# The head of a four-layer trunk: first transfers in small ordered pieces, squares later, constant products on TensorE first

## The chip, the cores and the metric

One Trainium2 chip, of which the kernel uses one core. The metric is the device time of one execution in microseconds (us), the median of several runs. TensorE multiplies matrices (its row is PE in the profile, and PEld for its loads of weights), VectorE (DVE) and ScalarE (ACT) do elementwise work, GpSimd (POOL) makes masks, SyncE (SP) issues most transfers.

## The reference

Two layers (`DEPTH = 2`) over 256 tokens of width 1024, all in float32. Each layer is a half-step SwiGLU, a mixer of three branches (sparse attention, pooling, state-space scan), a second half-step SwiGLU and an embedding gate. Only the start of the first half-step matters here:

```python
def rmsnorm(x, g):
    x32 = x.astype(jnp.float32)
    y = x32 * lax.rsqrt(jnp.mean(x32 * x32, axis=-1, keepdims=True) + EPS)
    return (y * g.astype(jnp.float32)).astype(x.dtype)

def swiglu(x, w_gate, w_up, w_down):
    return (jax.nn.silu(x @ w_gate) * (x @ w_up)) @ w_down

    h = x
    for i in range(DEPTH):
        h = h + 0.5 * swiglu(rmsnorm(h, ffn1_norm[i]), ffn1_w_gate[i], ffn1_w_up[i], ffn1_w_down[i])
        ...
    return rmsnorm(h, final_norm)
```

## The kernel before

The state `h` lies transposed, as 8 pieces of 128 channels x 256 tokens. A float32 product is made of three products of shortened numbers: every operand is split into a rounded part `hi` (ScalarE casts) and the rest `lo` (VectorE subtracts), and `mm3` (L161) issues hi x hi, lo x hi, hi x lo. The split activations are `uh` and `ul` (L187, L188), the split weights `whi` and `wlo` (L140, L141).

Weights come in units of 128 x 1024 numbers (512 KB). A unit has three buffers: `raw` (4 in turn), where the transfer lands, and `whi`, `wlo` (5 in turn each). So the transfer of unit n waits until the split of unit n-4 has read its `raw`, and the cast of unit n waits until TensorE is done with unit n-5. I count units from 0. One unit is 8 steps of `mm3`, 24 matmuls of 256 columns; units 2f and 2f+1 (gate and up) fill the two halves of one PSUM bank of `mm`, and there are 4 such banks, so the first matmul of unit 8 waits until the bank of units 0 and 1 has been read: once by `t = mm * r` (L369) and once more, after ScalarE's tanh (L371), by `t = t * mm` (L373).

The factor `r` of the norm comes aside: the squares of `h` are summed into `acc` (L218, L221, L223), TensorE sums `acc` over the channels with a product with `ones` (into `aux`), VectorE takes the inverse root in a chain of small operations (L250, `rsqrt` at L190) and writes two scaled identities (L256, L257), TensorE spreads them with `onesr` into another `aux`, and ScalarE copies that to `rs_r` (L267). Only then can a bank of `mm` be read. In the first half-step, matmuls run ahead of `r`.

In `build` (L1081) the first transfers are issued from SP: `h` in parts of 2, 2 and 4 pieces, and the first unit in two halves between them (`first`, L145); the two tables of gains `cc` go out from ScalarE's queue in `constants`. The squares of the first norm are asked for in `ffn` by `rnorm(late=True)` (L226). Within an engine, instructions are executed in the order of its queue. That order is made when the program is built, by a scheduler with its own estimate of times; `keep_in_program_order` holds an instruction to the order of the code, `turn` and `high_priority` push others.

Of the kernel before, what the change touches and what calls it, by code (L numbers as in the profile page):

```python
# [9 lines left out]
F = mybir.dt.float32  # L10
FR = mybir.dt.float32r
I32 = mybir.dt.int32
AF = mybir.ActivationFunctionType
OP = mybir.AluOpType
AX = mybir.AxisListType

P = 128
D = 1024
S = 256
DEPTH = 2  # L20
KD = D // P
# [24 lines left out]
NCC = -(-_n // 32) * 32  # L46
# [18 lines left out]
class Builder:  # L65
# [76 lines left out]
                                          op=OP.subtract))  # L142
        return hi, lo

    def first(self, c):  # L145

        nc = self.nc
        if c == 4:
            self.made.append(self.load(*self.order[1]))
            return  # L150
        if c == 0:
            self.start = self.parts()
            self.made.append(self.start[1:])
        layer, u, n = self.order[0]
        s = slice(0, 512) if c == 0 else slice(512, n)
        raw, hi, lo = self.start
        nc.sync.dma_start(raw[:, s], self.ins["w"][layer, u, :, s])
        nc.scalar.copy(hi[:, s], raw[:, s])  # L158
        nc.vector.tensor_tensor(lo[:, s], raw[:, s], hi[:, s].bitcast(F), op=OP.subtract)

    def mm3(self, ps, a, b, start, stop, keep=False):  # L161

# [47 lines left out]
            self.turn(nc.vector.scalar_tensor_tensor(y[:, :n], t[:, :n], 1.5, y[:, :n],  # L210
                                                     op0=OP.add, op1=OP.mult))

    def square(self, c, src, add=True):

        nc = self.nc
        if c == 0:
            self.acc = self.t([P, S], tag="acc", bufs=2)
            nc.scalar.activation(self.acc, src, AF.Square)  # L218
            return
        sq = self.t([P, S], tag="t1")  # L220
        nc.scalar.activation(sq, src, AF.Square)  # L221
        if add:
            nc.vector.tensor_tensor(self.acc, self.acc, sq, op=OP.add)  # L223
        else:
            self.last_sq = sq

    def rnorm(self, late=False, gap=1):

        nc = self.nc
        r = self.t([P, S], tag="rs_r", bufs=2)
        v = self.t([P, 2], tag="rs_v", bufs=2)
        rc = self.t([P, 8], tag="rs_y", bufs=2)
        acc = None if late else self.acc

        def steps():
            nonlocal acc
            if late:
                for c in range(KD):  # L240
                    self.square(c, self.h[:, c])
                    if c % 4 == 3:
                        yield
                acc = self.acc
            with self.tc.high_priority(offset=160):
                ps = self.bank("aux")
                for h in range(2):
                    self.mm(ps[:, h:h + 1], acc[:, h * P:(h + 1) * P], self.ones[:, :1],
                                     start=True, stop=True)
                self.turn(nc.vector.tensor_scalar(v, ps[:, :2], 1.0 / D, EPS, op0=OP.mult,  # L250
                                                  op1=OP.add))
                self.rsqrt(rc, v, 2)
                dh, dl = (self.t([P, 2, P], FR, tag="t1") for _ in range(2))
                for h in range(2):
                    x = rc[:, h:h + 1]
                    self.turn(nc.vector.tensor_scalar(dh[:, h], self.ident, x, None, op0=OP.mult))  # L256
                    self.turn(nc.vector.scalar_tensor_tensor(dl[:, h], self.ident, x,  # L257
                                                             dh[:, h].bitcast(F), op0=OP.mult,
                                                             op1=OP.subtract))
            for _ in range(gap):  # L260
                yield
            pr = self.bank("aux")
            for i, d in enumerate((dh, dl)):
                self.mm(pr[:, :S], self.onesr, d.rearrange("p a b -> p (a b)"),
                                 start=(i == 0), stop=(i == 1))
            with self.tc.high_priority(offset=160):
                nc.scalar.copy(r, pr[:, :S])  # L267

        self.todo = steps()
        return rc, r  # L270

# [5 lines left out]
    def constants(self):  # L277
        nc = self.nc
        c = self.const
        self.ident = c.tile([P, P], F, name="ident")  # L280
        self.ones = c.tile([P, P], F, name="ones")
        self.tri = c.tile([P, P], F, name="tri")
        self.up = c.tile([P, P], F, name="up")

        self.after = c.tile([P, 4, P], mybir.dt.bfloat16, name="after")
        nc.gpsimd.memset(self.ones, 1.0)
        nc.gpsimd.affine_select(out=self.ident, in_=self.ones, pattern=[[-1, P]],
                                compare_op=OP.is_equal, fill=0.0, base=0, channel_multiplier=1)

        nc.gpsimd.affine_select(out=self.tri, in_=self.ones, pattern=[[1, P]],  # L290
                                compare_op=OP.is_ge, fill=0.0, base=0, channel_multiplier=-1)
        nc.gpsimd.affine_select(out=self.up, in_=self.ones, pattern=[[-1, P]],
                                compare_op=OP.is_gt, fill=0.0, base=0, channel_multiplier=1)
        for i in range(4):
            nc.gpsimd.affine_select(out=self.after[:, i], in_=self.ones, pattern=[[1, P]],
                                    compare_op=OP.is_gt, fill=0.0, base=0, channel_multiplier=-1)
        self.onesr = c.tile([P, P], FR, name="onesr")
        nc.vector.tensor_copy(self.onesr, self.ones)

        warm = self.t([P, 1], tag="warm", bufs=1)  # L300
        nc.gpsimd.memset(warm, 0.0)
        nc.scalar.activation(warm, warm, AF.Tanh)
        self.cc = []
        for i in range(DEPTH):
            cc = c.tile([P, NCC], F, name=f"cc{i}")
            nc.scalar.dma_start(cc, self.ins["cc"][i])
            self.cc.append(cc)

    def col(self, layer, name, i=0, n=1):
        k = CC[name] + i  # L310
# [29 lines left out]
    def ffn(self, layer, u0, nxt, aside=None):  # L340
        nc = self.nc
        first = layer == 0 and u0 == U_FFN1
        _, r = self.rnorm(late=first, gap=3 if first else 2)
        gh = self.a([P, KF, S], FR, "gh")
        gl = self.a([P, KF, S], FR, "gl")
# [735 lines left out]
    def build(self):  # L1081
        nc = self.nc
        self.constants()
        self.h = self.const.tile([P, KD, S], F, name="h")
        self.a([P, LINE // 8], F, "shift")
        self.new_u()
        for c in range(KD):
            if c in (0, 2, 4):
                n = (2, 0, 2, 0, 4)[c]
                nc.sync.dma_start(self.h[:, c:c + n], self.ins["x"][:, c:c + n])  # L1090
                if self.order:
                    self.first(c)
            self.prep(c, 0, "ffn1_norm", False)
        for i in range(DEPTH):
            self.ffn(i, U_FFN1, (i, "mix_norm"))
            self.mix(i, (i, "ffn2_norm"))
            self.ffn(i, U_FFN2, (i, "ple_norm"), self.per_layer(i))
            self.ple(i, (i + 1, "ffn1_norm") if i + 1 < DEPTH else None)
# [109 lines left out]
```

## Time and profile before

| | us |
|---|---|
| median of 3 runs (1331.26 to 1332.53) | 1332.47 |
| the profiled execution | 1331.12 |
| its span, first to last instruction | 1329.4 |
| TensorE busy | 1308.3 |
| start of the first matmul | 6.62 |

The profiled execution took 1.35 us less than the median and 1.7 us more than its span. TensorE is busy in 98% of the span, so what counts is where it starts, waits, or runs at a lower clock. Times in the rows are from the start of the span.

### The profile page before, as it was taken

How to read it: one execution, taken by the hardware profiler on the slowest of the kernel's cores; microseconds unless marked ns; L12 is line 12 of the kernel's file. 1: busy time of each engine (PE TensorE's matmuls, PEld its weight loads, DVE VectorE, ACT ScalarE, POOL GpSimd, SP SyncE). 2: the span in 40 equal slices, each digit the busy share in tenths (PEclk: the TensorE clock that was granted, in tenths of full speed). 3: DMA queues.
4: the chain of work that ended last, by engine and by line, in shares of the span. 5: the costliest groups of instructions: out<-in, count | busy, mean ns of one | idle time of the engine just before them, and what ended most of it. 6: DMA issues, size and time to landing. Idle time of an engine off the chain costs nothing.

```text
span 1329.4 us, 28282 instructions
## 1 busy us (share of the span) xinstructions
PE 1308.3 (98%) x11502; PEld 1297.2 (98%) x11502; DVE 1040.5 (78%) x1971; ACT 740.9 (56%) x1209; POOL 7.0 (1%) x17
## 2 busy tenths in 40 slices
PE   7999999999999999999999999999999999999997
PEld 7999999999999999999999999999999999999997
DVE  7877659987989777766887776699789888777666
ACT  6555446656764555544645554566577546554454
POOL 0000000000000000000000000000000000000000
PEclk9999999999999999999999999999999999999999
DMA  7666656566637566666556666456655466666661
GB/s 255 209 193 193 192 168 206 159 203 195 188 122 230 159 222 191 193 194 197 187 164 192 193 194 196 155 195 192 198 187 163 151 207 206 193 195 198 193 192 47
DMA packets 72385, 248.24 MB, mean 187 GB/s; under 512 B 7936, under 2 KB 10304, under 8 KB 72256
## 3 DMA queue, kind: packets, MB, share of 16 engines
q1 hardware_dynamic: 71392, 245.17, 60.1%
q8 instruction: 90, 1.47, 0.5%
q10 hardware_dynamic: 864, 1.28, 0.3%
q14 instruction: 39, 0.32, 0.1%
HBM read 245.33 MB, written 1.08 MB: 185 GB/s over the span
## 4 chain that ended last, share of the span: by engine, by line
PE 95%; DVE 2%; DMA 1%; ACT 1%; issue 0%; DVEq 0%; ACTq 0%
PE mm L164 30%; PE mm L166 29%; PE mm L165 29%; PE aux L106 3%; PE aux L165 1%; PE aux L166 1%; DMA t<-in_p_dram 1%; PE aux L164 1%; PE aux L109 1%; DVE wlo L141 0%; ACT whi L140 0%; DMA h<-in_x_dram 0%; DVE ul L188 0%; DVE acc L223 0%; ACT uh L187 0%
## 5 line engine op out<-in xcount | busy, mean ns | idle before, releaser
L140 ACT CAST whi<-raw 128x1024 fp32r<-128x1024 f32 (+1 forms) x457 | 476.2, 1045 | 487.5 <-issue 234.6
L164 PE MATMUL mm<-uh,whi 128*128 128x256 f32 x2550 | 707.1, 279 | 8.7 <-ACT whi L158 6.6
L166 PE MATMUL mm<-uh,wlo 128*128 128x256 f32 x2560 | 709.2, 278 | 1.5 <-DVE wlo L141 1.5
L165 PE MATMUL mm<-ul,whi 128*128 128x256 f32 x2560 | 708.4, 277 | 0.4 <-DVE ul L188 0.3
L141 DVE TENSOR_TENSOR wlo<-raw,whi 128x1024 fp32r<-128x1024 f32 (+1 forms) x457 | 551.9, 1213 | 195.8 <-ACT whi L140 192.6
L164 PEld LDWEIGHTS mm<-uh,whi 128*128 128x128 f32 x2550 | 479.1, 189 | 11.5 <-ACT whi L158 6.6
L166 PEld LDWEIGHTS mm<-uh,wlo 128*128 128x128 f32 x2560 | 482.1, 188 | 2.8 <-DVE wlo L141 2.2
L165 PEld LDWEIGHTS mm<-ul,whi 128*128 128x128 f32 x2560 | 482.5, 189 | 1.1 <-DVE ul L188 1.1
L166 PE MATMUL mm<-gh,wlo 128*128 128x256 f32 x704 | 194.1, 276 | 0.0
L165 PE MATMUL mm<-gl,whi 128*128 128x256 f32 x704 | 194.1, 276 | 0.0
L164 PE MATMUL mm<-gh,whi 128*128 128x256 f32 x704 | 193.7, 276 | 0.0
L166 PEld LDWEIGHTS mm<-gh,wlo 128*128 128x128 f32 x704 | 132.1, 188 | 0.0
L165 PEld LDWEIGHTS mm<-gl,whi 128*128 128x128 f32 x704 | 132.1, 188 | 0.0
L164 PEld LDWEIGHTS mm<-gh,whi 128*128 128x128 f32 x704 | 131.8, 188 | 0.0
L165 PE MATMUL mm<-a,whi 128*128 128x256 f32 x256 | 70.3, 276 | 0.0
L164 PE MATMUL mm<-a,whi 128*128 128x256 f32 x256 | 70.2, 276 | 0.0
L166 PE MATMUL mm<-a,wlo 128*128 128x256 f32 x256 | 69.9, 277 | 0.0
L164 PEld LDWEIGHTS mm<-a,whi 128*128 128x128 f32 x256 | 47.9, 188 | 0.0
L165 PEld LDWEIGHTS mm<-a,whi 128*128 128x128 f32 x256 | 47.9, 188 | 0.0
L166 PEld LDWEIGHTS mm<-a,wlo 128*128 128x128 f32 x256 | 47.6, 188 | 0.0
L369 DVE TENSOR_TENSOR t<-mm,rs_r 128x256 f32<-128x256 f32 x88 | 37.3, 423 | 10.5 <-PE mm L166 0.9
L374 DVE SCALAR_TENSOR_TENSOR t<-t,t 128x256 f32<-128x256 f32 x88 | 37.4, 425 | 3.0
(213 smaller groups left out, 1106.0 us busy)
## 6 DMA issues: line engine op xcount, KB each, us to landing
raw<-in_w_dram SPq DMA_DIRECT2D x447, 512.0 KB, 4.2
gh<-rates SPq DMA_DIRECT2D x16, 256.0 KB, 4.4
raw<-in_w_dram SPq DMA_DIRECT2D x8, 352.0 KB, 3.0
raw<-in_w_dram SPq DMA_DIRECT2D x4, 256.0 KB, 3.8
gh<-rates SPq DMA_DIRECT2D x8, 128.0 KB, 3.6
h<-in_x_dram SPq DMA_DIRECT2D x2, 256.0 KB, 4.1
h<-in_x_dram SPq DMA_DIRECT2D x1, 512.0 KB, 5.7
t<-in_p_dram ACTq DMA_DIRECT2D x2, 256.0 KB, 5.8
```

What stands on the lines that cost most here:

```text
L106: self.tc.keep_in_program_order(self.nc.tensor.matmul(*args, **kw))
L109: self.tc.keep_in_program_order(self.nc.tensor.transpose(*args))
L140: nc.scalar.copy(hi[:, :n], raw[:, :n])
L141: self.turn(nc.vector.tensor_tensor(lo[:, :n], raw[:, :n], hi[:, :n].bitcast(F), op=OP.subtract))
L164: (self.mm if keep else mm)(ps, a[0], b[0], start=start, stop=False)
L165: mm(ps, a[0], b[1], start=False, stop=False)
L166: mm(ps, a[1], b[0], start=False, stop=stop)
L369: nc.vector.tensor_tensor(t, p1[0], r, op=OP.mult)
L374: nc.vector.scalar_tensor_tensor(g, th, 1.0, t, op0=OP.add, op1=OP.mult)
```

## The change

The transfers of the first 4 us are cut into a list, `HEAD`, of ten pieces: single pieces of `h` (128 KB) and then pairs, and units 0 and 1 in parts of 256 and 512 columns. `head` issues them in that order, from SP except the first weights, which go out from ScalarE's queue beside 32 columns of `cc` (the gains of the first norm); the rest of `cc` follows after the ten. The casts and splits are held to the same order on ScalarE and VectorE. The squares are held to the code's order, which puts them behind these. 15 products of the constant `onesr` with itself stand first in TensorE's queue; nothing reads their result.

```diff
-    def first(self, c):
-        ...
+    HEAD = (("x", 0, 1), ("w", 0, 0, 256), ("x", 1, 1), ("w", 0, 256, 512), ("x", 2, 2),
+            ("w", 0, 512, 1024), ("x", 4, 2), ("x", 6, 2), ("w", 1, 0, 512), ("w", 1, 512, 1024))
+
+    def head(self, layer, gain):
+        nc = self.nc
+        keep = self.tc.keep_in_program_order
+        units = [self.parts() for _ in range(2)] if self.order else []
+        self.made = [u[1:] for u in units]
+        for k, (what, i, *n) in enumerate(self.HEAD):
+            if what == "x":
+                i = slice(i, i + n[0])
+                keep(nc.sync.dma_start(self.h[:, i], self.ins["x"][:, i]))
+            elif units:
+                s = slice(*n)
+                queue = nc.scalar if k == 1 else nc.sync
+                keep(queue.dma_start(units[i][0][:, s], self.ins["w"][layer, self.order[i][1], :, s]))
+            if k == 1:
+                keep(nc.scalar.dma_start(self.cc[0][:, :32], self.ins["cc"][0, :, :32]))
+        ...
+        for what, i, *n in self.HEAD:
+            if what == "x":
+                for c in range(i, i + n[0]):
+                    g = self.col(layer, gain, c)
+                    hi, lo, src = self.uh[:, c], self.ul[:, c], self.h[:, c]
+                    keep(nc.scalar.mul(hi, src, g))
+                    keep(nc.vector.scalar_tensor_tensor(lo, src, g, hi.bitcast(F),
+                                                        op0=OP.mult, op1=OP.subtract))
+            elif units:
+                raw, hi, lo = (x[:, slice(*n)] for x in units[i])
+                keep(nc.scalar.copy(hi, raw))
+                keep(nc.vector.tensor_tensor(lo, raw, hi.bitcast(F), op=OP.subtract))
+
+        keep(nc.sync.dma_start(self.cc[0][:, 32:], self.ins["cc"][0, :, 32:]))
+        for i in range(1, DEPTH):
+            keep(nc.sync.dma_start(self.cc[i], self.ins["cc"][i]))
     ...
+    def square(self, c, src, add=True, keep=False):
     ...
-                    self.square(c, self.h[:, c])
+                    self.square(c, self.h[:, c], keep=True)
     ...
-        self.cc = []
-        for i in range(DEPTH):
-            cc = c.tile([P, NCC], F, name=f"cc{i}")
-            nc.scalar.dma_start(cc, self.ins["cc"][i])
-            self.cc.append(cc)
+        ps = self.bank("aux")
+        for _ in range(15):
+            nc.tensor.matmul(ps[:, :P], self.onesr, self.onesr, start=True, stop=True)
+        self.cc = [c.tile([P, NCC], F, name=f"cc{i}") for i in range(DEPTH)]
     ...
-        for c in range(KD):
-            if c in (0, 2, 4):
-                n = (2, 0, 2, 0, 4)[c]
-                nc.sync.dma_start(self.h[:, c:c + n], self.ins["x"][:, c:c + n])
-                if self.order:
-                    self.first(c)
-            self.prep(c, 0, "ffn1_norm", False)
+        self.head(0, "ffn1_norm")
```

Since the scheduler places the rest, other instructions move too. After about 180 rows of TensorE's queue and 60 of VectorE's and ScalarE's the order is the one of before. Three places matter. In the rows the numbers name buffers.

TensorE's queue, the sum of squares. Before, the product with `ones` stands after three units and ahead of unit 3 (`whi_149`), 73 rows ahead of the products with `onesr`:

```order
L165 MATMUL mm_237<-ul_100,whi_143 128x256
L166 MATMUL mm_237<-uh_99,wlo_144 128x256
L106 MATMUL aux_268<-ones,acc_184 128x1 x2
L164 MATMUL mm_237<-uh_99,whi_149 128x256
L165 MATMUL mm_237<-ul_100,whi_149 128x256
```

Of the change, the same product stands ahead of the last matmul of unit 5 (`wlo_222`):

```order
L188 MATMUL mm_347<-uh_110,whi_221 128x256
L189 MATMUL mm_347<-ul_111,whi_221 128x256
L106 MATMUL aux_293<-ones,acc_209 128x1 x2
L190 MATMUL mm_347<-uh_110,wlo_222 128x256
L188 MATMUL mm_439<-uh_110,whi_264 128x256
```

It moved back by nearly three units. The products with `onesr` moved back by one unit only, from the start of unit 6 to within the first step of unit 7 (`whi_318`, `wlo_319`):

```order
L188 MATMUL mm_439<-uh_110,whi_318 128x256
L189 MATMUL mm_439<-ul_111,whi_318 128x256
L106 MATMUL aux_408<-t_45_311,onesr 128x256
L106 MATMUL aux_408<-t_46_312,onesr 128x256
L190 MATMUL mm_439<-uh_110,wlo_319 128x256
```

So 27 matmuls lie between the two products, where 72 did.

VectorE's queue behind the chain of the inverse root, before: the last of the two scaled identities, the splits of units 7 to 10, then the two operations that read the bank of units 0 and 1 (`mm_141`):

```order
L257 SCALAR_TENSOR_TENSOR t_45_287<-ident,rs_y_138,t_44_286 128x128
L141 TENSOR_TENSOR wlo_294<-raw_292,whi_293 128x1024
L141 TENSOR_TENSOR wlo_325<-raw_323,whi_324 128x1024
L141 TENSOR_TENSOR wlo_355<-raw_353,whi_354 128x1024
L141 TENSOR_TENSOR wlo_417<-raw_415,whi_416 128x1024
L369 TENSOR_TENSOR t_57_387<-mm_141,rs_r_136 128x256
L373 TENSOR_TENSOR t_57_387<-t_57_387,mm_141 128x256
```

Of the change, the bank of units 0 and 1 is `mm_166`:

```order
L285 SCALAR_TENSOR_TENSOR t_46_312<-ident,rs_y_163,t_45_311 128x128
L141 TENSOR_TENSOR wlo_319<-raw_317,whi_318 128x1024
L141 TENSOR_TENSOR wlo_350<-raw_348,whi_349 128x1024
L141 TENSOR_TENSOR wlo_380<-raw_378,whi_379 128x1024
L141 TENSOR_TENSOR wlo_442<-raw_440,whi_441 128x1024
L393 TENSOR_TENSOR t_58_412<-mm_166,rs_r_161 128x256
L141 TENSOR_TENSOR wlo_472<-raw_470,whi_471 128x1024
L397 TENSOR_TENSOR t_58_412<-t_58_412,mm_166 128x256
```

The splits of units 7 to 10 stand behind the chain in both; the split of unit 11 (`wlo_472`) has moved between the two readers of the bank.

ScalarE's queue at the same place, before: the copy of `rs_r`, the first tanh, then the cast of unit 11 (`whi_446`):

```order
L140 CAST whi_416<-raw_415 128x1024
L267 COPY rs_r_136<-aux_383 128x256
L371 ACTIVATE t_58_389<-t_57_387 128x256
L140 CAST whi_446<-raw_445 128x1024
L183 CAST gh_139<-t_59_391 128x256
```

Of the change:

```order
L295 COPY rs_r_161<-aux_408 128x256
L140 CAST whi_471<-raw_470 128x1024
L395 ACTIVATE t_59_414<-t_58_412 128x256
L140 CAST whi_511<-raw_510 128x1024
L207 CAST gh_164<-t_60_416 128x256
```

The cast of unit 11 has moved ahead of the first tanh.

## Rows read from the trace of the kernel before

**Rows 1.** The page: span, shares of the chain by engine, and casts of the weights.

```profile
span 1329.4 us, 28282 instructions
...
PE 95%; DVE 2%; DMA 1%; ACT 1%; issue 0%; DVEq 0%; ACTq 0%
...
L140 ACT CAST whi<-raw 128x1024 fp32r<-128x1024 f32 (+1 forms) x457 | 476.2, 1045 | 487.5 <-issue 234.6
```

**Rows 2.** Timeline, 0 to 17 us: start, length, engine, line, operation, [idle before <-releaser].

```profile
4.54 0.42 ACT L218 ACTIVATE acc<-h 128x256 f32<-128x256 f32 x1 [1.80 <-DMA h<-in_x_dram]
...
5.97 0.60 ACT L158 CAST whi<-raw 128x512 fp32r<-128x512 f32 x1
...
6.60 0.69 DVE L159 TENSOR_TENSOR wlo<-raw,whi 128x512 fp32r<-128x512 f32 x1
6.62 0.58 PE L164 MATMUL mm<-uh,whi 128*128 128x256 f32 x1 [6.62 <-ACT whi L158]
...
9.47 1.66 DVE L188 SCALAR_TENSOR_TENSOR ul<-h,cc,uh 128x256 fp32r<-128x256 f32 x4
...
11.05 2.01 DVE L223 TENSOR_TENSOR acc<-acc,t 128x256 f32<-128x256 f32 x4
...
12.08 0.41 PE L165 MATMUL mm<-ul,whi 128*128 128x256 f32 x1
...
12.72 0.41 PE L165 MATMUL mm<-ul,whi 128*128 128x256 f32 x1
12.97 4.62 DVE L141 TENSOR_TENSOR wlo<-raw,whi 128x1024 fp32r<-128x1024 f32 x4
...
14.25 0.39 PE L166 MATMUL mm<-uh,wlo 128*128 128x256 f32 x1 [1.11 <-DVE wlo L141]
```

**Rows 3.** The page: transfers by line, count, KB each, median us from issue to landing.

```profile
raw<-in_w_dram SPq DMA_DIRECT2D x447, 512.0 KB, 4.2
...
rates<-t SPq DMA_DIRECT2D x2, 16.0 KB, 2.1
```

**Rows 4.** Line 139 alone, 4.7 to 4.8 us: the transfer of unit 2.

```profile
DMA to landing us min/median/max: 6.3/6.3/6.3
```

**Rows 5.** Line 139 alone, 27 to 28 us: the transfer of unit 11.

```profile
DMA to landing us min/median/max: 3.5/3.5/3.5
```

**Rows 6.** Timeline of VectorE, 18 to 37 us.

```profile
22.48 0.15 DVE L250 TENSOR_SCALAR rs_v<-aux 128x2 f32<-128x2 f32 x1
...
26.06 4.62 DVE L141 TENSOR_TENSOR wlo<-raw,whi 128x1024 fp32r<-128x1024 f32 x4
30.60 0.42 DVE L369 TENSOR_TENSOR t<-mm,rs_r 128x256 f32<-128x256 f32 x1
31.50 0.42 DVE L373 TENSOR_TENSOR t<-t,mm 128x256 f32<-128x256 f32 x1 [0.48 <-ACT t L371]
```

**Rows 7.** Timeline of TensorE, 28 to 34 us: units 6 and 7, and unit 8's first matmul.

```profile
28.23 0.40 PE L106 MATMUL aux<-t,onesr 128*128 128x256 f32 x2
28.47 0.28 PE L164 MATMUL mm<-uh,whi 128*128 128x256 f32 x1
...
33.94 0.28 PE L164 MATMUL mm<-uh,whi 128*128 128x256 f32 x1
```

**Rows 8.** Timeline, 197 to 198 us: a later norm, where VectorE was idle.

```profile
197.04 0.50 PE L106 MATMUL aux<-ones,acc 128*128 128x1 f32 x4
197.40 0.41 PE L106 MATMUL aux<-whi,uh 128*128 128x344 f32 x1
197.58 0.16 DVE L250 TENSOR_SCALAR rs_v<-aux 128x2 f32<-128x2 f32 x1 [2.71 <-PE aux L106]
```

**Rows 9.** Timeline of TensorE, 665 to 674 us.

```profile
670.31 0.58 PE L106 MATMUL aux<-ones,acc 128*128 128x1 f32 x4 [1.87 <-DVE acc L223]
```

**Rows 10.** Stretches: length, PE, PEld, DVE, ACT, POOL busy (instructions), PEclk (granted clock), DMA.

```profile
672.00:675.00 3.00, 3.00 (x16) 3.00 (x16) 2.75 (x12) 1.26 (x2) 0.00 (x0) 0.50 0.00 0
675.00:676.00 1.00, 1.00 (x9) 1.00 (x8) 1.00 (x2) 0.03 (x1) 0.00 (x0) 0.86 0.00 0
```

More of the change, by code (lines that the diff above doesn't have):

```diff
@@ L143, in load @@
         return hi, lo
-    def first(self, c):
+    HEAD = (("x", 0, 1), ("w", 0, 0, 256), ("x", 1, 1), ("w", 0, 256, 512), ("x", 2, 2),
+            ("w", 0, 512, 1024), ("x", 4, 2), ("x", 6, 2), ("w", 1, 0, 512), ("w", 1, 512, 1024))
+    def head(self, layer, gain):
         nc = self.nc
[L148 to L159, printed above, removed]
+        keep = self.tc.keep_in_program_order
[11 more added lines that the diff above has]
+                keep(nc.scalar.dma_start(self.cc[0][:, :32], self.ins["cc"][0, :, :32]))
+        warm = self.t([P, 1], tag="warm", bufs=1)
+        nc.gpsimd.memset(warm, 0.0)
+        keep(nc.scalar.activation(warm, warm, AF.Tanh))
+        for what, i, *n in self.HEAD:
[13 more added lines that the diff above has]
+            keep(nc.sync.dma_start(self.cc[i], self.ins["cc"][i]))
@@ L211, in rsqrt @@
                                                      op0=OP.add, op1=OP.mult))
-    def square(self, c, src, add=True):
+    def square(self, c, src, add=True, keep=False):
         nc = self.nc
@@ L217, in square @@
             self.acc = self.t([P, S], tag="acc", bufs=2)
-            nc.scalar.activation(self.acc, src, AF.Square)
+            ins = nc.scalar.activation(self.acc, src, AF.Square)
+            if keep:
+                self.tc.keep_in_program_order(ins)
             return
         sq = self.t([P, S], tag="t1")
-        nc.scalar.activation(sq, src, AF.Square)
+        ins = nc.scalar.activation(sq, src, AF.Square)
+        if keep:
+            self.tc.keep_in_program_order(ins)
         if add:
@@ L298, in constants @@
         nc.vector.tensor_copy(self.onesr, self.ones)
-        warm = self.t([P, 1], tag="warm", bufs=1)
-        nc.gpsimd.memset(warm, 0.0)
-        nc.scalar.activation(warm, warm, AF.Tanh)
-        self.cc = []
-        for i in range(DEPTH):
-            cc = c.tile([P, NCC], F, name=f"cc{i}")
-            nc.scalar.dma_start(cc, self.ins["cc"][i])
-            self.cc.append(cc)
+        ps = self.bank("aux")
+        for _ in range(15):
+            nc.tensor.matmul(ps[:, :P], self.onesr, self.onesr, start=True, stop=True)
+        self.cc = [c.tile([P, NCC], F, name=f"cc{i}") for i in range(DEPTH)]
     def col(self, layer, name, i=0, n=1):
```

## The prediction

> **What bounds the kernel now.** I read the page first. The chain that ended last runs 95% through TensorE [rows 1], and 1308.3 of the 1329.4 us of the span are matmuls; work on another engine counts only where TensorE waits for it. So the question is narrow: at which time does TensorE stand at a place behind which nothing changes? The order of the queues gives that place. Behind the first matmul of unit 8 all engines do what they did before, and in the trace of before TensorE reaches it at 33.94 us without a wait [rows 7]. I compare that moment.
>
> Next the timeline of the first 17 us [rows 2]. The first two pieces of `h` end ScalarE's wait at 4.54; the first matmul starts at 6.62, released by the cast of half a unit. Then matmuls of 256 columns start 0.213 us apart (three from 12.08 to 12.72): that is the lower of TensorE's two levels, 1.2 GHz. At 14.25 TensorE, which had done 26 matmuls, ends a wait of 1.11 us for the `lo` part of unit 1: VectorE had eight splits of `h`, two of weights and seven sums of squares to do before that. From then on it runs at the upper level: the 48 matmuls of units 6 and 7 take 33.94 - 28.47 = 5.47, 0.114 each [rows 7]. 26 matmuls at that rate are 3.0 us; so 14.25 - 3.0 = 11.3 us of the head are lost. That is all that the change can get at.
>
> **What the change gains: the first operands.** Half as many bytes stand ahead of the first pair, and no square stands ahead of the first cast. No row shows a landing of 128 KB: 16 KB landed in 2.1 us [rows 3], the first 256 KB by 4.51, 3.7 after their issue at 0.80. I take 3.4, so landing at 4.2 (bounds 2.9 and 4.5). One scaling and one cast of 256 columns follow, about 0.8 together (half a unit's cast is 0.60 [rows 2]); the first matmul starts near 5.1. The 15 constant products need nothing but `onesr`, ready at about 1.3, and a product of 128 columns can hardly exceed the 0.213 of 256 columns; at that they end at 4.5, in time, and cost nothing.
>
> For the same thing the Trainium skill has a rule against small pieces, in "DMA: Bandwidth & Descriptors", sections "Anatomy of one DMA" and "Rules for kernel authors": about 2.0 us fixed plus bytes at 436 GB/s, measured on GpSimd's path, so that transfers should be merged. The trace does not agree for the first one (2.6 by the rule, 3.7 here). By the rule 128 KB would land at 3.1 and the forecast would be lower by at most 0.6, since the next step sets a floor.
>
> **What bounds the gain: VectorE, then the transfer of unit 2.** With the seven sums gone from the front, VectorE has eight splits of `h` at 0.395 (four from 9.47 to 11.05), three halves of a unit at 0.61 (0.69 alone [rows 2], the next one overlaps its end) and two quarters at some 0.34: 5.7 us from 4.7, so unit 1 is split at about 10.4 instead of 14.20. But unit 2 has the same bytes ahead of it as before (all of `h`, `cc`, units 0 and 1), and before it landed at 4.71 + 6.3 = 11.0 [rows 4]. Its cast (1.05 [rows 1]) and split (1.2, as from 12.97 to 14.25 [rows 2]) end at 13.3. TensorE then has 50 matmuls behind it, and the product with `ones` is 93 further on: 13.4 + 93 x 0.114 = 24.0. That is the early bound. The late one: if the clock rises no sooner than before (after 12.72), unit 0 ends near 10.5, 12 more matmuls are done by 13.1, and the other 107 take 12.2: 25.3. I call this moment S and take S = 24.6. The squares are no limit: the last thing queued ahead of them is the split of unit 6, whose transfer follows the split of unit 2 at 13.3 and needs 3.5 to 4.2, so they are done by about 21. Unit 6 starts at S + 0.47 = 25.1, where before it started at 28.47: a lead of 3.4 us.
>
> **What the change gives back: the chain of the norm.** The order puts the product with `ones` nearly three units later and all that follows from it close behind. From S:
> - VectorE starts the chain 0.54 after the product's start (197.04 to 197.58 [rows 8]) and needs 22.48 to 26.06 = 3.58 [rows 6]. It was idle until then, with the split of unit 7 queued behind the chain. The products with `onesr` can start at S + 4.2. TensorE arrives after 0.36 (197.04 to 197.40) and 27 matmuls, at S + 3.44: a wait of 0.8.
> - The split of unit 7 starts at S + 4.12 and ends at S + 5.34; TensorE has finished `onesr` (0.24 [rows 7]) at S + 4.45 and waits 0.9. Before, 24 more matmuls of unit 6 covered this.
> - 22 matmuls bring it to unit 8 at S + 7.86. There it needs the bank of units 0 and 1. VectorE first does the other three splits (all four take 30.60 - 26.06 = 4.54), reads the bank once at S + 8.66, and then stands at the split of unit 11, which the change has moved ahead of the second reading. Unit 11 can be sent only when the split of unit 7 has freed its buffer, at S + 5.34; 3.5 us later it lands [rows 5], at S + 8.86. Cast 1.05, split 1.15 to the next start, the second reading 0.42 [rows 6]: S + 11.6. The tanh between is behind the same cast and done by then. TensorE waits 3.7.
>
> Unit 8 starts at S + 11.6 = 36.2, where before it was 33.94: 2.3 late (1.7 to 3.0 by S; at the median landing of 4.2 [rows 3] it is 0.7 more). The lead of 3.4 has turned into a lag, since 5.4 us of waits are new. Before, the whole chain lay beside 72 matmuls, and unit 11's split behind the second reading.
>
> **The clock.** A wait of 3.7 us has its own price. At 670.31 TensorE ended a wait of 1.87 us [rows 9], and from 672 on its granted clock was 0.50, the lower level, until some 0.28 us into the next row, although it was busy again [rows 10]. The wait of 1.11 at 14.25 had no such effect. 3.3 us at half rate cost 1.6. I take that once; it may be up to twice that if a second low stretch follows, and nothing if the clock holds.
>
> **Sum.** + 2.3 + 1.6 = + 3.9 on the profiled execution's 1331.12: 1335.0. That execution was 1.35 below the median of the runs, so against the median of 1332.47 I forecast + 2.5, or 0.19%. A difference of 0.2%, 2.7 us, is about what a measurement of this kernel can tell from none: the forecast lies on that line, with a lean to slower.
>
> **Rivals.**
> 1. The bank's first half is enough. If unit 8 waits only for the first reading, it starts at S + 8.66 + 0.42 + 0.05 = S + 9.1 = 33.7, after a wait of 1.3, near the 1.11 that left the clock alone: 1330.9, no change. For it: unit 8 writes only that half. Against it: in the changed order unit 9, which writes the other half, has no wait on VectorE of its own, so unit 8's must cover both.
> 2. The constant does not do what it is said to. It ends before the first real matmul, and the matmuls of unit 0 come no faster than ScalarE and VectorE feed them, so the clock may stay low until 13, S is 25.3, and after the long wait two low stretches follow: 36.9 - 33.94 + 3.3 = 6.3, 1337.4, slower.
> 3. The lead is kept. One mechanism decides: if the waits between S and unit 8 sum to under 0.5, the 3.4 us of lead stay, 1327.7, faster by 0.4%. For it: VectorE is idle for some 3 us ahead of S, so there is room for the splits of units 7 to 10. Against it: they are queued behind the chain, and an engine keeps its queue's order. It starts to be faster than before when the new waits fall below 3.4.
>
> **Chances.** The forecast 0.55 (half of it above the line), rival 1 0.13, rival 2 0.19, rival 3 0.13. Slower 0.27 + 0.19 = 0.46, same 0.28 + 0.13 = 0.41, faster 0.13. The forecast's own range is 1333 to 1337.5 (S, the landing, the clock). With half of rival 3's neighbourhood left out below and little above, 1329.5 to 1338.5 holds eight in ten.
>
> **What would show it.** First matmul of unit 0 near 5.1 and `lo` of unit 1 by 11; product with `ones` between 24.0 and 25.3; VectorE idle for the 3 us before it; TensorE's wait for L397 at unit 8 of about 3.7, with a granted clock of 0.50 behind it; unit 8 near 36. A wait under 1 us there, or a start of unit 8 before 33, makes the forecast wrong; a start near 36 without the low clock makes its second term wrong.

## The result and the profile after

The changed kernel takes 1339.34 us (median of 6 runs, 1335.72 to 1340.33) where the kernel before took 1331.88 beside it (6 runs): a ratio of 1.0052, 95% interval 1.0041 to 1.0063. It is slower by some 7.5 us; forecast were 2.5, and a range that ended at 1338.5. The profiled execution took 1338.62, 7.50 more than the profiled one of before.

The page of the changed kernel begins like that of before [rows 1]: TensorE still carries nearly all of the chain, so the question is again where TensorE waited, and at which clock it ran. (Lines are shifted: the three products of `mm3` are L188 to L190 here, the first reading of a bank L393, the second L397.)

```profile
span 1336.8 us, 28326 instructions
...
PE 95%; DVE 2%; DMA 2%; ACT 1%; issue 0%; SPq 0%; DVEq 0%; ACTq 0%
```

The timeline of TensorE in the changed kernel answers to [rows 2] and [rows 7]: start, length, engine, line, operation, and in brackets the idle time before it with what ended it.

```profile
1.31 3.46 PE L330 MATMUL aux<-onesr 128*128 128x128 f32 x15 [1.31 <-DVE onesr L326]
5.24 0.58 PE L188 MATMUL mm<-uh,whi 128*128 128x256 f32 x1 [0.46 <-ACT whi L178]
8.16 0.58 PE L188 MATMUL mm<-uh,whi 128*128 128x256 f32 x1 [1.15 <-ACT uh L173]
...
10.59 0.58 PE L189 MATMUL mm<-ul,whi 128*128 128x256 f32 x1
10.97 0.41 PE L190 MATMUL mm<-uh,wlo 128*128 128x256 f32 x1
11.18 0.41 PE L188 MATMUL mm<-uh,whi 128*128 128x256 f32 x1
...
14.38 0.41 PE L188 MATMUL mm<-uh,whi 128*128 128x256 f32 x1
14.60 0.37 PE L189 MATMUL mm<-ul,whi 128*128 128x256 f32 x1
14.80 0.28 PE L190 MATMUL mm<-uh,wlo 128*128 128x256 f32 x1
...
27.44 0.50 PE L106 MATMUL aux<-ones,acc 128*128 128x1 f32 x4
31.31 0.77 PE L106 MATMUL aux<-t,onesr 128*128 128x256 f32 x2 [0.19 <-DVE t L284]
32.83 0.39 PE L190 MATMUL mm<-uh,wlo 128*128 128x256 f32 x1 [0.75 <-DVE wlo L141]
39.10 0.58 PE L188 MATMUL mm<-uh,whi 128*128 128x256 f32 x1 [3.48 <-DVE t L397]
```

Read it from the end. The last row is the first matmul of unit 8. It starts at 39.10, 5.16 later than before [rows 7], after a wait of 3.48 us for the second reading of its bank. S, the product with `ones`, starts at 27.44. Further up, the starts of the matmuls are 0.213 us apart from 10.97 to 14.60 and some 0.115 from there on: by this spacing the lower of the two levels lasted until 14.6. The column PEclk, the granted clock, reads 1.00 there too (from 11 to 14 us); in run 15 below, from 38.4 to 42.6 us, it reads 0.50 with the same spacing of 0.213. So in the head the level can be read from the spacing alone.

Between 8.16 and 31.31 no row has a bracket. Up to 10.97 the starts are still up to 0.53 apart, while ScalarE and VectorE deliver the operands of unit 0 piece by piece: these are waits too short for a bracket. From 10.97 to 31.31 TensorE waited for nobody, neither for VectorE nor for the transfer of unit 2.

The chain of waits of the changed kernel (start, length, what) shows why unit 8 waits, step by step:

```profile
27.60 0.35 PE aux L106 x4
27.98 0.17 DVE rs_v L278
...
31.06 0.21 DVE t L284
31.56 1.23 DVE wlo L141
32.80 3.53 DMA raw<-in_w_dram
36.41 1.05 ACT whi L140
37.49 1.09 DVE wlo L141
38.63 0.42 DVE t L397
39.10 0.58 PE mm L188
```

The small operations of the norm, the split of unit 7, which frees a buffer, the transfer of unit 11 into it, its cast, its split, and only then the reading for which unit 8 waits.

Toward the end of the wait the granted clock falls, and it stays low behind it, in the changed kernel's stretches (columns as in [rows 10]; the last is the GB/s moved):

```profile
36.00:38.00 2.00, 0.00 (x0) 0.00 (x0) 1.03 (x3) 1.36 (x2) 0.00 (x0) 1.00 0.67 238
38.00:39.00 1.00, 0.00 (x0) 0.00 (x0) 1.00 (x2) 0.40 (x1) 0.00 (x0) 0.84 0.88 344
39.00:42.00 3.00, 2.90 (x13) 2.90 (x14) 2.23 (x5) 1.37 (x3) 0.00 (x0) 0.50 0.99 376
42.00:43.00 1.00, 1.00 (x11) 1.00 (x10) 0.97 (x4) 0.05 (x2) 0.00 (x0) 0.96 0.46 152
```

13 matmuls in the three us at 0.50, where the upper level does 26: that is 1.5 us. To see the loss of the head alone, I take a landmark far behind it, the issue of the first transfer of `p` (first row before, second row after):

```profile
428.48 0.33 ACTq L395 DMA_DIRECT2D t<-in_p_dram  x1
```

```profile
435.28 0.33 ACTq L419 DMA_DIRECT2D t<-in_p_dram  x1
```

6.80 us late: 5.16 at unit 8 and 1.64 behind it, nearly all of it the clock. The other 0.70 of the 7.50 come behind the landmark, where both kernels do the same; I did not follow them.

### The profile page after: what moved, and what is told of

It is laid out like the page before. It is cut to its first block, busy times and chain, and to the rows that moved or that the text cites. A ratio compares the mean times of both kernels' runs of the same rounds, so it can differ in the third digit from the quotient of the medians.

```text
span 1336.8 us, 28326 instructions
## 1 busy us (share of the span) xinstructions
PE 1315.5 (98%) x11517; PEld 1303.1 (97%) x11517; DVE 1041.0 (78%) x1973; ACT 742.2 (56%) x1211; POOL 7.0 (1%) x17
## 4 chain that ended last, share of the span: by engine, by line
PE 95%; DVE 2%; DMA 2%; ACT 1%; issue 0%; SPq 0%; DVEq 0%; ACTq 0%
PE mm L188 30%; PE mm L190 29%; PE mm L189 29%; PE aux L106 3%; PE aux L189 1%; PE aux L190 1%; DMA t<-in_p_dram 1%; PE aux L188 1%; PE aux L109 1%; DVE wlo L141 1%; ACT whi L140 0%; DMA h<-in_x_dram 0%; DMA raw<-in_w_dram 0%; DVE acc L251 0%; DVE rs_t L232 0%
## 5 line engine op out<-in xcount | busy, mean ns | idle before, releaser
L188 PE MATMUL mm<-uh,whi 128*128 128x256 f32 x2550 | 708.0, 279 | 6.9 <-DVE t L397 3.5
L190 PE MATMUL mm<-uh,wlo 128*128 128x256 f32 x2560 | 709.9, 278 | 1.2 <-DVE wlo L141 1.2
L188 PEld LDWEIGHTS mm<-uh,whi 128*128 128x128 f32 x2550 | 479.7, 189 | 10.7 <-DVE t L397 3.7
L190 PEld LDWEIGHTS mm<-uh,wlo 128*128 128x128 f32 x2560 | 483.1, 189 | 2.2 <-DVE wlo L141 1.8
L190 PE MATMUL mm<-gh,wlo 128*128 128x256 f32 x704 | 194.1, 276 | 0.0
L188 PE MATMUL mm<-gh,whi 128*128 128x256 f32 x704 | 193.7, 276 | 0.0
L190 PEld LDWEIGHTS mm<-gh,wlo 128*128 128x128 f32 x704 | 132.2, 188 | 0.0
L188 PEld LDWEIGHTS mm<-gh,whi 128*128 128x128 f32 x704 | 131.9, 188 | 0.0
L188 PE MATMUL mm<-a,whi 128*128 128x256 f32 x256 | 70.2, 276 | 0.0
L190 PE MATMUL mm<-a,wlo 128*128 128x256 f32 x256 | 69.9, 277 | 0.0
L188 PEld LDWEIGHTS mm<-a,whi 128*128 128x128 f32 x256 | 47.9, 188 | 0.0
L190 PEld LDWEIGHTS mm<-a,wlo 128*128 128x128 f32 x256 | 47.6, 188 | 0.0
L393 DVE TENSOR_TENSOR t<-mm,rs_r 128x256 f32<-128x256 f32 x88 | 37.2, 423 | 10.5 <-PE mm L190 1.1
```

The lines of the kernel that those rows point to most:

```text
L188: (self.mm if keep else mm)(ps, a[0], b[0], start=start, stop=False)
L190: mm(ps, a[1], b[0], start=False, stop=stop)
L393: nc.vector.tensor_tensor(t, p1[0], r, op=OP.mult)
```

## The experiments

All are compared with the kernel before on the same chip. "Landmark" is the issue of the transfer of `p` in the run's profiled execution against that of the kernel before, in us; N is the number of matmuls of units 0 to 7 that TensorE does ahead of S. A landmark is one execution against one; three of the changed kernel itself lie at +6.28, +6.80 and +7.12.

| run | us | ratio to before, 95% | N | S | landmark |
|---|---|---|---|---|---|
| changed kernel | 1339.34 | 1.0041 to 1.0063 | 143 | 27.44 | +6.80 |
| 1 squares free | 1332.36 | 1.0001 to 1.0020 | 72 | 19.09 | -0.30 |
| 2 old pieces | 1336.81 | 1.0030 to 1.0055 | 136 | 25.20 | +4.57 |
| 3 no constants | 1338.63 | 1.0043 to 1.0069 | 143 | 26.03 | +6.74 |
| 4 reading first | 1332.40 | 0.9999 to 1.0016 | 143 | 25.68 | +0.32 |
| 5 both moves, old pieces | 1331.91 | 0.9992 to 1.0009 | 120 | 23.97 | -1.10 |
| 6 both moves, new pieces | 1330.64 | 0.9983 to 1.0000 | 120 | 24.71 | -0.24 |
| 7 forty constants | 1333.63 | 1.0003 to 1.0021 | 100 | 23.94 | +1.81 |
| 8 changed, again | 1339.16 | one run | 143 | 26.39 | +7.12 |
| 9 only the squares | 1336.16 | 1.0024 to 1.0049 | 130 | 24.71 | +5.30 |
| 10 only the constants | 1330.97 | 0.9989 to 1.0006 | 72 | 19.44 | -0.18 |
| 11 `ones` early | 1333.16 | 1.0009 to 1.0026 | 120 | 23.88 | +1.65 |
| 12 whole `cc` on run 6 | 1329.41 | 0.9976 to 0.9995 | 120 | 22.49 | -2.55 |
| 13 changed, whole `cc` | 1339.60 | 1.0035 to 1.0061 | 143 | 26.20 | +5.66 |
| 14 run 12 again | 1330.96 | 0.9986 to 1.0004 | 120 | 22.99 | -1.99 |
| 15 changed, third | 1338.83 | one run | 143 | 25.87 | +6.28 |

### Which part of the change costs: runs 1, 9, 10, 2 and 3

Run 1, the squares no longer held in order:

```diff
-                    self.square(c, self.h[:, c], keep=True)
+                    self.square(c, self.h[:, c])
```

> The changed kernel, but the squares of the first norm are not held in the order written (the scheduler puts the product with `ones` back behind unit 3, `onesr` behind unit 6). Theory A (the late norm chain makes the waits): the waits of 0.75, 0.19 and 3.48 us after `ones` go, the granted clock does not fall behind them, unit 8 starts at 33.4 to 34.5 us as in the kernel before, and the time is 1331 to 1333. Theory B (the slow first transfers alone make the loss, the place of the chain is innocent): unit 8 stays near 39 and the time near 1338.

1332.36, with `ones` behind 72 matmuls again and no bracket at unit 8. Theory A holds: of 7.5 us less than one is left, with the small pieces, the strict order of casts and splits, and the constants all in place.

Run 9 is the other direction: the kernel before, and only its squares held in order (`keep=True` in `square` as in the change).

> The kernel before with one part of the change: the squares of the first norm held in the order written. `ones` comes 57 matmuls later than before. Theory A (that alone makes the loss): S at 24 to 26, a wait of 3 us or more at unit 8, unit 8 at 35.8 to 37.6, a granted clock of 0.50 behind it, time 1335.5 to 1339. Rival (VectorE, free of the sums in front, splits unit 1 so much earlier that it pays): 1332.5 or less.

1336.16, landmark +5.30. Its timeline has the same wait, and its stretches the same low clock:

```profile
24.71 0.50 PE L106 MATMUL aux<-ones,acc 128*128 128x1 f32 x4
...
36.27 0.58 PE L164 MATMUL mm<-uh,whi 128*128 128x256 f32 x1 [3.34 <-DVE t L377]
```

```profile
38.00:42.00 4.00, 4.00 (x21) 4.00 (x21) 3.65 (x10) 1.88 (x5) 0.00 (x0) 0.50 0.68 245
```

So the late squares alone make most of the loss. What the rest of the change adds (1.0 to 1.8 at the landmark) would fit N: `ones` comes behind 143 matmuls there and behind 130 here, and 13 x 0.114 are 1.5. No run takes this remainder apart.

Run 10 is the kernel before with the 15 constant products alone.

```diff
+        ps = self.bank("aux")
+        for _ in range(15):
+            nc.tensor.matmul(ps[:, :P], self.onesr, self.onesr, start=True, stop=True)
```

> The kernel before with another part alone: the 15 constant products. They end near 4.8 us, before the first operand (6.6). Theory C: nothing changes, 1331.3 to 1332.8, first matmul at 6.6 and spaced 0.213. Rival (they raise the clock for the first matmuls): 1330 or less.

1330.97: no difference. Run 3 takes the same lines out of the changed kernel.

> The changed kernel without the 15 constant products. Theory C (they end before the first operand and do not raise the clock): first matmul at 5.2, spacing 0.213 until about 14.6, time within 1.5 us of the changed kernel (1338 to 1340.5). Rival (they help the clock): the low level lasts longer and the time is 2 us or more above; rival (they are in the way): 1337 or less.

1338.63, again none. Run 2 keeps the order of the change and sends the pieces of before:

```diff
-    HEAD = (("x", 0, 1), ("w", 0, 0, 256), ("x", 1, 1), ("w", 0, 256, 512), ("x", 2, 2),
-            ("w", 0, 512, 1024), ("x", 4, 2), ("x", 6, 2), ("w", 1, 0, 512), ("w", 1, 512, 1024))
+    HEAD = (("x", 0, 2), ("w", 0, 0, 512), ("x", 2, 2), ("w", 0, 512, 1024), ("x", 4, 4), ("w", 1, 0, 1024))
...
-                queue = nc.scalar if k == 1 else nc.sync
+                queue = nc.sync
```

> The changed kernel, but with the six pieces of the kernel before (x in 2, 2, 4 parts, unit 0 in two halves, unit 1 whole, all on SP's queue); only the 16 KB of `cc` stay on ScalarE's. Theory B (small pieces make the first transfers slow): the first matmul is later (6.0 to 6.6), but unit 2 lands at 11 to 12 instead of 13.2, the product with `ones` starts at 24 to 25.5 instead of 27.4, unit 8 at 35.6 to 37.1, and the time is 1335 to 1337. Rival (the transfers are slow because of what is sent, not of its pieces): `ones` at 27 or later, 1339 or more.

S at 25.20, unit 8 at 36.79 and 1336.81, as theory B said. But the scheduler had also put `ones` 7 matmuls further forward, and the clock rose at 9.7 us in this profile. So theory B's numbers came out, but runs 5, 6 and 13 speak against its reason.

### Which place behind S costs: runs 4, 11, 5 and 6

Run 4 moves the second reading of the bank of units 0 and 1 ahead of the splits of units 10 and 11. (It writes another tile, so that it need not wait for the tanh.)

```diff
+                    if first and f1 == 0:
+                        self.turn(nc.vector.tensor_tensor(g, t, p1[1], op=OP.mult))
+                        t = g
+                    else:
                         nc.vector.tensor_tensor(t, t, p1[1], op=OP.mult)
```

> The changed kernel, but the second reading of the bank of units 0 and 1 writes another tile and stands ahead of the splits of units 10 and 11 on VectorE. Theory A: the wait of 3.48 us at unit 8 becomes about 1.4, unit 8 starts at 37.0 instead of 39.1, the clock does not fall to 0.50 behind it, and the time is 1335 to 1336.5. Rival (the wait only moves to the next bank or the next split): a wait of 2 us or more at unit 9 or 10, time 1338 or more.

1332.40, below what theory A expected. The wait is all but gone, and so is the low clock behind it:

```profile
25.68 0.50 PE L106 MATMUL aux<-ones,acc 128*128 128x1 f32 x4
...
31.08 0.39 PE L190 MATMUL mm<-uh,wlo 128*128 128x256 f32 x1 [0.75 <-DVE wlo L141]
34.23 0.36 PE L188 MATMUL mm<-uh,whi 128*128 128x256 f32 x1 [0.33 <-DVE t L398]
```

```profile
36.00:44.00 8.00, 8.00 (x73) 8.00 (x73) 7.73 (x14) 5.88 (x11) 0.00 (x0) 1.00 0.87 315
```

I had put the new wait at 1.4, since I overlooked that the split of unit 10 moves behind the readings too: the first one starts at S + 7.53 here, not at S + 8.66. Two splits ahead of one reading are worth some 6 to 7 us (6.0 to 6.8 at the landmark).

Run 11 leaves that place and only queues `ones` 23 matmuls earlier:

```diff
                     w = self.unit(layer, u0 + 2 * f + j, 1024)
+                    with ExitStack() as stack:
+                        if first and (f, j) >= (2, 1):
+                            stack.enter_context(self.tc.issue_after(self.summed.ins))
                         self.mmk([(ps[j], w)], u, keep=f == 1 and j == 0)
```

> The changed kernel with `ones` queued ahead of unit 5 (23 matmuls earlier), the second bank reading left where the change has it. Theory A: S at 23.8 to 24.9, the waits of 0.19 and 0.75 go, that at unit 8 falls only to 2.0 to 2.6 (the transfer of unit 11 still ends it), unit 8 at 35.2 to 36.8, 1334 to 1337. Rival (the place of `ones` is all): wait under 1, 1332 or less. Rival (the reading is all): 1338 or more.

1333.16, a little better than theory A's lower end. The waits of 0.19 and 0.75 are gone, and 2.56 are left at unit 8, as worked out; but this wait left the clock alone:

```profile
35.51 0.39 PE L188 MATMUL mm<-uh,whi 128*128 128x256 f32 x1 [2.56 <-DVE t L402]
```

```profile
35.50:40.00 4.50, 4.49 (x39) 4.49 (x40) 3.80 (x8) 2.77 (x6) 0.00 (x0) 1.00 0.90 303
```

Runs 5 and 6 make both moves, with the old and with the new pieces.

> The old pieces, the second bank reading ahead of the splits of units 10 and 11, and the product with `ones` queued ahead of unit 5 (24 matmuls earlier than the changed kernel has it; VectorE was idle for 3 to 4.6 us there). Theory A (all the loss behind S is the place of the norm chain and of the second reading): S near 23.3, no wait over 0.5 us between it and unit 8, unit 8 at 32 to 32.5 where the kernel before has 33.9, time 1329 to 1331. Rival (the chain only waits elsewhere, for the sums of squares): S at 24.5 or later with a wait in front, unit 8 at 34 or later, 1332 or more.

> The same two moves with the small pieces of the changed kernel. Theory B (small pieces cost, in unit 2's landing and through it): 1 to 2 us above the version with the old pieces, unit 8 at 32.3 to 34. Rival (the pieces are worth their earlier first matmul): equal to it or below.

1331.91 and 1330.64: the new pieces are not slower, and theory B's 1 to 2 us don't show. There is no bracket between S and unit 8 in either, and unit 8 starts at S + 8.9. Theory A is not met in full: run 5 has S at 23.97 for 23.3 and unit 8 at 32.87 for 32 to 32.5, and its time is that of the kernel before, where 1329 to 1331 was expected.

### What sets S: runs 7, 13, 8, 15, 12 and 14

Run 7 has 40 constants for 15 (`range(40)`).

> The changed kernel with 40 constant products in place of 15. They end near 10.5 us and delay the first real matmul to there. Theory C1 (constant products don't raise the clock): they keep their spacing of 0.23 to the end, the real matmuls start at 0.213 and the time is 3 us or more above the changed kernel (1342 or more). Theory C2 (15 were too few, a longer stretch raises it): the spacing falls to 0.12 or less before they end, the real matmuls run at the upper level from their start, S is 25 to 27 and the time 1337 to 1340.

Neither theory's time: 1333.63. What C1 says of the clock holds. TensorE has no idle time from 1.32 us on, and the level still changes only at 14.9:

```profile
1.32 8.80 PE L330 MATMUL aux<-onesr 128*128 128x128 f32 x40 [1.32 <-DVE onesr L326]
9.92 0.52 PE L188 MATMUL mm<-uh,whi 128*128 128x256 f32 x1
...
14.72 0.41 PE L189 MATMUL mm<-ul,whi 128*128 128x256 f32 x1
14.93 0.33 PE L190 MATMUL mm<-uh,wlo 128*128 128x256 f32 x1
15.10 0.28 PE L188 MATMUL mm<-uh,whi 128*128 128x256 f32 x1
...
23.94 0.58 PE L106 MATMUL aux<-ones,acc 128*128 128x1 f32 x4
```

It is faster than the changed kernel for a reason that I had not foreseen: the longer constant made the scheduler queue `ones` behind 100 matmuls instead of 143. So S came earlier although every matmul came later. Unit 8 starts at S + 11.73, as it does in the changed kernel (S + 11.66), but TensorE has 43 more matmuls to do behind S and waits only 0.30.

Run 13 makes the first transfers of the changed kernel faster. Of the gains `cc`, the change sends 16 KB in rows of 128 bytes first and the rest last; here both tables go out whole on ScalarE's queue, as before. With that, the rest of `cc` no longer stands ahead of unit 2 on SP's queue. The order of the engines behind the head stays the same.

```diff
-                keep(nc.scalar.dma_start(self.cc[0][:, :32], self.ins["cc"][0, :, :32]))
+                for i in range(DEPTH):
+                    keep(nc.scalar.dma_start(self.cc[i], self.ins["cc"][i]))
...
-        keep(nc.sync.dma_start(self.cc[0][:, 32:], self.ins["cc"][0, :, 32:]))
-        for i in range(1, DEPTH):
-            keep(nc.sync.dma_start(self.cc[i], self.ins["cc"][i]))
```

> The changed kernel with `cc` sent whole on ScalarE's queue and nothing else altered; the order of all engines behind the head is the changed kernel's. Theory D (the transfers are the larger part of the error in S): S at 24 to 25.3 as forecast, unit 8 at S + 11.7 = 35.7 to 37, and 1335 to 1337.5, 2 to 4 us under the changed kernel. Rival (the clock's rise is the larger part, and the transfers only hide behind it): S at 26 or later, 1338 or more.

The transfers are faster: 189 GB/s from 4 to 7 us in the changed kernel (first row), 326 in run 13 (second row; the last column).

```profile
4.00:7.00 3.00, 2.54 (x10) 2.03 (x9) 1.64 (x4) 1.62 (x4) 0.00 (x0) 1.00 0.83 189
```

```profile
4.00:7.00 3.00, 2.35 (x10) 2.03 (x9) 1.61 (x4) 1.74 (x5) 0.00 (x0) 1.00 1.00 326
```

Unit 2's cast starts at 11.43 where it was 13.23 (12.5 in runs 8 and 15). That is not the rate but the issue. SP's rows of the changed kernel (first fence) and of run 13 (second) have it at 7.60, behind the two pieces of `cc`, and at 5.86; from issue to landing it took 5.6 in both.

```profile
5.49 0.65 SPq L181 DMA_DIRECT2D cc<-in_cc_dram  x1
6.18 0.65 SPq L183 DMA_DIRECT2D cc<-in_cc_dram  x1
7.60 1.27 SPq L139 DMA_DIRECT2D raw<-in_w_dram  x2
```

```profile
5.86 0.80 SPq L139 DMA_DIRECT2D raw<-in_w_dram  x2
```

And the earlier data do not bring S forward:

```profile
5.43 0.58 PE L186 MATMUL mm<-uh,whi 128*128 128x256 f32 x1 [0.65 <-ACT whi L179]
7.44 0.58 PE L186 MATMUL mm<-uh,whi 128*128 128x256 f32 x1 [0.23 <-ACT uh L174]
...
13.47 0.29 PE L187 MATMUL mm<-ul,whi 128*128 128x256 f32 x1
...
26.20 0.50 PE L106 MATMUL aux<-ones,acc 128*128 128x1 f32 x4
...
37.91 0.58 PE L186 MATMUL mm<-uh,whi 128*128 128x256 f32 x1 [3.50 <-DVE t L395]
```

S is at 26.20, and the median 1339.60 (four executions at 1339.5 to 1339.8 and two at 1335.1; the changed kernel has one of six there, at 1335.72). Theory D falls, its rival holds: TensorE was at its lower level until 13.4 and could not use the earlier data. Run 8 below, whose level rose at 13.4 too, has S 0.19 later.

Runs 8 and 15 are the changed kernel unaltered, in two more profiles.

> The changed kernel unaltered, for a second profile. If the late rise of the clock (14.6 us) and S = 27.4 belong to that execution: rise between 11 and 13, S 25.5 to 26.3, unit 8 at 37.1 to 38, span 1335 or less. If they belong to the program: 14 or later and S above 27 again.

> The changed kernel a third time (14.6 and 13.4 us for the rise so far, S 27.4 and 26.4). If the execution decides: a rise before 13 or after 15. If the program does: 13 to 15 again. The low stretch behind the wait at unit 8 was about 3.3 and 6.6 us long; one of these two lengths again.

The level rose at 13.4, between the two cases of run 8, and at 12.1, so the execution has a large say. Over the profiles of kernels with N = 143, S follows the rise: 27.44 for 14.6 us, 26.39 and 26.20 for 13.4, 26.03 for 12.7 (run 3), 25.87 for 12.1, 25.68 for 11.6 (run 4). The low stretch at the wait differs as well: by the granted clock of the rows it lasted some 3.4 us in the first profile and 6.8 in runs 8 and 15, as run 15 expected. The wait covers its beginning; TensorE worked in it for 3.0, 6.1 and 5.3 us. The rows of run 8:

```profile
38.00:40.00 2.00, 1.99 (x9) 1.99 (x10) 1.38 (x2) 0.58 (x1) 0.00 (x0) 0.50 0.97 373
...
42.00:44.00 2.00, 2.00 (x12) 2.00 (x11) 1.74 (x5) 1.30 (x3) 0.00 (x0) 0.50 0.45 182
```

Run 12 puts the whole `cc` on run 6, and run 14 repeats it.

> Run 6 with the constants `cc` sent whole on ScalarE's queue, as in the kernel before, instead of 16 KB there and the rest last on SP's. Theory D (the piece of 128-byte rows is what holds the transfers at 107 to 234 GB/s from 4 to 7 us): 300 GB/s or more there, `h` 2 and 3 landed by 7.1 instead of 7.7, time 0.5 to 1.5 us below run 6. Rival (rows of 1 KB do it): below 250 GB/s again, time within 0.7 of run 6 or above, since `cc` lands later.

> Run 12 once more. Its time: 1328.5 to 1330.5, below the kernel before in every comparison. The rise of the clock: near 10.3 again if it belongs to the program; anywhere from 9.7 to 14.9, and S then up to 2 us later, if it belongs to the execution.

355 GB/s from 4 to 7 us, but `cc` lands later: the first matmul starts only at 6.77, 1.5 us behind the changed kernel's, and yet this version has the lowest median, with the landmark 2.55 and 1.99 early.

```profile
6.77 0.58 PE L186 MATMUL mm<-uh,whi 128*128 128x256 f32 x1 [1.99 <-ACT whi L179]
...
22.49 0.50 PE L274 MATMUL aux<-ones,acc 128*128 128x1 f32 x4
```

1329.41 beat the kernel before by 0.05 to 0.24%; the repetition (1330.96) missed its 1328.5 to 1330.5, and its interval holds no difference. Against the kernel before on the same chip, run 12 gained 2.0 us, run 14 0.4 and run 6 1.5. Sure is that it beats the changed kernel, by some 8 to 9 us. Whether the whole `cc` has a part in it stays open: the level rose at 10.3 and 11.7 us here against 14.7 in run 6, and each us at the lower level costs 0.46 (a matmul takes 0.213 there and 0.1145 above), so that alone is worth more than the 1.2 us between run 12 and run 6.

## Why the prediction was wrong

The direction was right, and so was the mechanism behind S, nearly to the row. From S the forecast was: VectorE's chain after 0.54, the first reading at S + 8.66, unit 8 at S + 11.6. In the trace they are 27.98 - 27.44 = 0.54, 8.66 (L393 at 36.10) and 11.66. In all nine profiles in which the second reading stands behind the split of unit 11 (the changed kernel and runs 2, 3, 7, 8, 9, 11, 13 and 15), unit 8 starts at S + 11.56 to S + 11.74. Of the three waits, 0.8, 0.9 and 3.7, came 0.19 (and 0.2 more between the two products with `onesr`), 0.75 and 3.48. Runs 1, 4 and 9 show the cause: take away either the late `ones` or the split between the two readings, and the loss is gone; put the late squares into the kernel before, and it is there.

The clock's term was 1.6 and "up to twice that": it was 1.64 in the profiled execution, and 3.0 and 2.6 in runs 8 and 15 (the landmark less unit 8). Rival 2 had priced two low stretches; run 8 has the length of two. It came nearest of the three, with 1337.4, but its S of 25.3 is 2.1 short too.

The step that failed is S, in the part on what bounds the gain: "13.4 + 93 x 0.114 = 24.0", taken as 24.6, late bound 25.3. It was 27.44, and 2.84 of the 3.62 us by which the profiled execution exceeds the forecast of 1335.0 are this term; 0.70 came behind the landmark. The step says that TensorE has 50 matmuls behind it at 13.4, because unit 2's data would be the bound. It had begun 26. 24 missing matmuls at 0.1145 are 2.7 us, which puts S at 26.7; the rest is the level, low until 14.6. At 0.213 from 5.24 on, TensorE could have begun 39 by 13.4 without any wait: 11 of the 24 are the lower level, and 13 are waits, the one at 8.16 and the short ones up to 10.97.

So I took the wrong bound. I asked when unit 2 would be there, and at 13.4 TensorE had only begun unit 1 and waited for nothing until 31.31. Unit 2 was 2.2 us later than forecast itself (13.2 for 11.0): I had counted the bytes ahead of it and not the issues, and SP came to it at 7.60 where it was 4.71 before. But this did not matter. Run 13 shows it by experiment, since unit 2 came 1.1 to 1.8 us earlier than in the three profiles of the changed kernel and S stayed within the spread of the other profiles. What bounded the first 14 us was TensorE itself: first its start, since the pieces 2 and 3 of `h`, there only at 7.6, made it wait 1.15 at 8.16, then the lower level, at 0.213 for each matmul. The late bound of 25.3 had a rise "no sooner than before (after 12.72)" in it, but counted unit 0 as done by 10.5, 24 matmuls; there were 13 to 17 in the profiles of this head (the changed kernel and runs 3, 4, 8 and 15). Even with a rise at 12.1, S was 25.87.

A second step made the forecast smaller still: the sum puts + 3.9 on the profiled execution of before and then compares with the median of before, so that 1.35 us drop out. Both profiled executions lie some 0.7 below their medians in the result (1331.12 and 1331.88, 1338.62 and 1339.34). Like against like, the forecast was + 3.9 where 7.5 came.

Of the transfers I had said that half the bytes ahead of the first pair would bring it sooner. They did, by 1.38 us (5.24 against 6.62 [rows 2]), close to the forecast 5.1. But by 10.5 us TensorE had begun 13 matmuls in the changed kernel and 15 before: the earlier start was spent in the waits for the next pieces. The bytes behind it moved at 189 GB/s from 4 to 7 us.

The Trainium skill says in "DMA: Bandwidth & Descriptors", "Why small descriptors are slow (HBM only)", that every packet and every descriptor has a fixed cost, which weighs on short rows. The runs do not show this as the cause of the rate. With the 128-byte rows of `cc` ahead, 189 GB/s moved in run 6 and 224 in run 15, and without them 355 and 326 in runs 12 and 13; but runs 2 and 5, with the same rows and the old pieces, moved 307 and 257. The time of the changed kernel did not depend on the rate (1339.34 and 1339.60).

The constants were counted as costing nothing and, in rival 2, as doing nothing: runs 3, 10 and 7 bear out both.

## What to carry to other kernels

When a piece of work is moved later in a queue, follow everything that its result releases and look for the buffer or bank that is freed last; here one reading queued behind a split, whose transfer waited for a buffer, cost some 6 us, where the new head with both moves gained 1.5 (run 6). Ask for each stretch which engine is the bound in it, at the clock it has there: here earlier data were worth 0.2 us to a TensorE that was busy at its lower level (run 13 against run 8). When transfers are cut into pieces, count the issues ahead of each one as well as the bytes. And a scheduler that places work by its own estimates can move a distant instruction when anything ahead of it changes, so compare the order before reading a run as the test of one edit.

## What was not expected of the hardware

- The moment at which TensorE's level rises in the head differs between executions of one program: 14.6, 13.4 and 12.1 us in three profiles of the changed kernel. Work ahead of it did not bring it forward: with 40 constant products, and no idle time from 1.32 us on, it rose at 14.9; in run 2, whose first matmul of unit 0 starts at 6.09, at 9.7. What decides it stays open. The granted clock of the profile reads 1.00 all through the head, also where the spacing of the matmuls is that of the lower level.
- A wait of 2.56 us (run 11) left the granted clock at 1.00, waits of 3.3 to 3.5 us were followed by 0.50, and so was one of 1.87 in the kernel before [rows 9, 10]. The length of one wait alone does not tell whether the clock falls. The same wait of 1.87 or 1.88 stands in other profiles too: over 665 to 690 us the granted clock is 0.93 in those of the kernel before and the changed one, 0.86 in runs 4 and 13, and 1.00 in run 14. This moves a single execution by some 1.7 us either way (0.07 of 25 us), behind the landmark.
- The low stretch that follows is not of one length: 3.4, 6.8 and 6.8 us at 0.50 at the same wait of one program, of which 3.0, 6.1 and 5.3 us were work.
